# Stick-breaking heads 4 to 6: scores as two matmuls over stacked high and low parts instead of three over masked ones

## The chip, the cores and the metric

The kernel runs on one core of a Trainium2 chip. The metric is the device time of one execution in microseconds. Three timed executions of the kernel before took 2678.01, 2680.74 and 2683.67 us; the median is 2680.74 us. The engines are named as in the profile: PE (matmul; PEld is its weight load), DVE (vector), ACT (scalar), POOL (GpSimd) and SP (the queue from which nearly all transfers are issued).

## The reference, cut to what matters

One layer of a transformer-like block over 2048 rows of width 1024. A normed input is projected; half of the mix is a differential attention with 4 heads, the other half a stick-breaking attention with 8 heads of width 64; then an output projection and a SwiGLU layer follow. The change touches how the scores `z` of the stick-breaking half are formed:

```python
def stick_breaking_attention(q, k, v):
    scale = SB_DIM ** -0.5                       # SB_DIM = 64
    z = jnp.einsum('bqhd,bkhd->bhqk', qb, k).astype(jnp.float32) * scale
    mask = (k_pos[None, :] < q_pos[:, None])[None, None]
    log_1mb = jnp.where(mask, jax.nn.log_sigmoid(-z), 0.0)
    rem = lax.cumsum(log_1mb, axis=3, reverse=True) - log_1mb
    a = jnp.where(mask, jnp.exp(jax.nn.log_sigmoid(z) + rem), 0.0)
    return jnp.einsum('bhqk,bkhd->bqhd', a.astype(v.dtype), v)
...
u = rms_norm(h, norm1_w[l])
proj = jnp.einsum('bsd,de->bse', u, w_in[l])     # diff q|k|v, then stick-breaking q|k|v
...
h = h + jnp.einsum('bse,ed->bsd', mix, w_out[l])
h = h + SwiGLU(rms_norm(h, norm2_w[l]))
```

All is float32. The kernel keeps that precision with float16 matmuls: each operand is split into a high half and a low half (the rounding rest), and a product is the sum of high·high, high·low and low·high.

## The kernel before, in words

The first phase works through eight groups `g` of 128 columns. Groups 0 to 3 are the differential heads, one per group; groups 4 to 7 hold two stick-breaking heads each, `m` = 0 and 1, on the partition halves 0 to 63 and 64 to 127. For each group 16 row tiles are projected (`proj`), and then (`sb_attn`) 16 query tiles `i` run over the keys before them, in chunks `sc` of up to 512 keys, 80 chunks a group. The projections of a group lie beside the attention of the group before it and the first half of its own. A second phase is the SwiGLU layer, which is nearly all matmul.

Groups 4 to 6 are "turned" (`turned(g)`, L330): their q and k leave the projection already transposed, with the 128 columns of both heads on the partitions and the rows along the free side. `proj_turned` (L334) puts q and k of two row tiles into one PSUM tile `pq` and v into `pv`. After each second row tile `turned_out` (L346) evacuates them: for each head q is multiplied by a column of `half`, which is 2^-11 on that head's partitions and zero on the other head's, into a high part (ACT, L350), and DVE takes the low part (L351). k is split once for both heads into high and low (`split_psum`, L359: the high part on ACT or DVE, whichever has the smaller count in `load`; the low part on DVE, L364), and v likewise. Because q is zero on the other head's partitions, a matmul over all 128 partitions gives one head's score. A chunk of scores (`score_chunk`, L504) is then three matmuls into one PSUM bank: q high·k high, q low·k high, q high·k low.

Group 7 and groups 0 to 3 take another way. Their q and k are transposed by transfers (L410), and a second transfer (L412) copies each half of `qT` to the other half of the partitions, so that high and low lie stacked over 128 partitions. For them a chunk of scores is two matmuls.

Behind the scores of a chunk, ACT takes two sigmoids (L619, L620), DVE a running product (L622) and a product (L623, on POOL for every second chunk of a longer row); ACT casts the result to a high half `s` (L89), POOL takes the low half (L98), and a transposing transfer on SP (L461) brings it into `aT`, which is the weight of the value matmuls (L518). The score tiles `sc` have 4 PSUM buffers, `s` has 3 buffers beside two spare kinds, `pq` and `pv` share the 2 buffers of `pj`, `qT` has 4 (`QB`) and `kT` 7 (`KB`).

The order on each engine is not written out. The framework's scheduler sorts all instructions by priority (attention ahead by 200, projection behind by 200) and a modelled course of time; every engine, and SP, then works through its own list in order. So a change in one place moves instructions in others.

## Time and profile before

| | |
|---|---|
| median of three runs | 2680.74 us (2678.01 to 2683.67) |
| span of the profiled execution | 2680.8 us, 50579 instructions |
| attention of groups 4, 5, 6 | about 600 to 757, 757 to 915 and 915 to 1085 us |
| attention of group 7 and part of the output projection | about 1085 to 1355 us |
| second phase | from about 1400 us on |

The span reaches from the first to the last instruction of the profiled execution. The page gives no other time of that execution; its span stands 0.1 us above the median of the timed runs, so nothing is added for what lies around it. The busy time of an engine is the union of its instructions. A matmul's end is modelled: it holds the time until its result is out, while the next matmul starts earlier, so the distance from start to start is what PE needs for one.

### The profile page before, as it was taken

To read this page: it belongs to the slowest core of one execution; us is meant where nothing else is said; L and a number is where in the kernel's file an instruction comes from. 1 tells how busy PE (TensorE), PEld (TensorE's weight loads), DVE (VectorE), ACT (ScalarE), POOL (GpSimd) and SP (SyncE) were. 2 spreads that over 40 slices of the span, in tenths; PEclk is the share of its full clock that TensorE was granted. 3 is DMA by queue.
4 is the path that set the end of the run, shared out by engine and by line. 5 is a ranking of instruction groups with operands and counts; after the bars stand their busy time and mean duration, and the time that the engine had idled before them with its cause. 6 is when DMAs were issued, how large, how long until landed. Compare 5 with 4: busy or idle time off the path is not lost. (4 is left out here: it accounts for less than half of the span.)

```text
span 2680.8 us, 50579 instructions
## 1 busy us (share of the span) xinstructions
PE 2492.4 (93%) x19628; PEld 1498.6 (56%) x19628; DVE 1932.7 (72%) x3711; ACT 1347.0 (50%) x2487; POOL 1489.1 (56%) x1098
## 2 busy tenths in 40 slices
PE   6998989888988989889989899999999999999999
PEld 4655656577776776557775344444444444444444
DVE  6898969898989989877766868777685544444434
ACT  4665656567978878665644535344352112111121
POOL 2578667667767766546764656565564232322323
PEclk9999999999999999999999899999999999999999
DMA  6777697767998979987897574665649743635532
GB/s 222 213 162 181 146 200 168 179 143 184 193 179 179 185 160 209 210 191 217 218 285 282 208 250 178 255 226 202 245 183 346 293 177 143 233 141 186 195 111 95
DMA packets 619585, 534.41 MB, mean 199 GB/s; under 512 B 480640, under 2 KB 548224, under 8 KB 609104
## 3 DMA queue, kind: packets, MB, share of 16 engines
q1 hardware_dynamic: 617520, 529.09, 69.9%
q8 instruction: 154, 2.52, 0.4%
q0 software_dynamic: 512, 1.36, 0.2%
q14 instruction: 87, 0.71, 0.1%
q10 hardware_dynamic: 1312, 0.72, 0.1%
HBM read 261.08 MB, written 147.32 MB: 152 GB/s over the span
## 5 line engine op out<-in xcount | busy, mean ns | idle before, releaser
L98 POOL TENSOR_TENSOR s<-z,s 128x1024 f16<-128x1024 f32 (+7 forms) x288 | 472.0, 1647 | 142.5 <-ACT s L89 109.8
L507 PE MATMUL sc<-kT,qT 128*128 128x512 f16 (+3 forms) x1520 | 382.0, 353 | 53.3 <-DVE z L623 19.3
L622 DVE TENSOR_TENSOR_SCAN z<-z,sc 128x512 f32<-128x512 f32 (+3 forms) x320 | 352.8, 1112 | 58.6 <-ACT sc L620 38.0
L1138 PE MATMUL pd<-wd,act 128*128 128x512 f16 x1764 | 390.9, 379 | 1.2 <-DVE cg L1071 1.2
L326 PE MATMUL pj<-w,xt 128*128 128x384 f16 x1920 | 352.2, 331 | 18.8 <-ACT xt L683 6.9
L1030 PEld LDWEIGHTS <-wg 128*128 128x128 f16 x1848 | 182.0, 99 | 230.2 <-issue 16.4
L518 PE MATMUL yp<-v,aT 128*128 128x64 f16 (+1 forms) x4896 | 269.8, 204 | 41.6 <-DMA aT<-s 40.2
L518 PEld LDWEIGHTS <-aT 128*128 128x128 f16 x4896 | 237.5, 99 | 120.4 <-DMA aT<-s 52.5
L1030 PEld LDWEIGHTS <-wu 128*128 128x128 f16 x1848 | 180.7, 98 | 218.0 <-issue 2.6
L98 POOL TENSOR_TENSOR act<-cg,act 128x512 f16<-128x512 f32 x112 | 148.5, 1337 | 262.9 <-ACT act L1097 150.8
L1138 PEld LDWEIGHTS <-act 128*128 128x128 f16 x1764 | 172.8, 98 | 209.4 <-issue 2.8
L326 PEld LDWEIGHTS <-xt 128*128 128x128 f16 x1920 | 187.3, 99 | 147.5 <-issue 21.4
L89 ACT CAST s<-z 128x128 f16<-128x128 f32 (+7 forms) x215 | 173.1, 809 | 134.1 <-DMA aT<-s 40.5
L98 POOL TENSOR_TENSOR hs<-hs,cu 128x512 f32<-128x512 f32 x99 | 130.9, 1328 | 171.3 <-DVE hs L1144 70.8
L619 ACT ACTIVATE z<-sc,c 128x512 f32<-128x512 f32 (+3 forms) x320 | 210.7, 663 | 25.6 <-PE sc L507 11.7
L1097 ACT CAST act<-cg 128x512 f16<-128x512 f32 x126 | 77.3, 616 | 238.4 <-DVE cg L1103 162.7
L507 PEld LDWEIGHTS <-qT 128*128 128x128 f16 x1520 | 128.4, 99 | 121.0 <-DVE z L623 23.0
L832 PE MATMUL po<-wo,mt 128*128 128x256 f16 x1536 | 180.7, 277 | 13.9 <-DVE xf L835 8.4
L1030 PE MATMUL pm<-X,wu 128*128 128x512 f16 x792 | 180.4, 379 | 1.3 <-DVE wu L221 1.3
L1030 PE MATMUL pm<-X,wg 128*128 128x512 f16 x792 | 181.3, 382 | 0.0
L342 PE MATMUL pj<-xt,w 128*128 128x128 f16 x2304 | 175.0, 220 | 6.7 <-DVE v L364 5.7
L1144 DVE SCALAR_TENSOR_TENSOR hs<-pd,c,hs 128x512 f32<-128x512 f32 x136 | 99.0, 747 | 109.6 <-PE pd L1138 83.1
(266 smaller groups left out, 4737.6 us busy)
## 6 DMA issues: line engine op xcount, KB each, us to landing
xt<-xs SPq DMA_DIRECT2D x112, 512.0 KB, 4.3
hs<-hd SPq DMA_DIRECT2D x68, 512.0 KB, 4.5
hd<-hs SPq DMA_DIRECT2D x56, 512.0 KB, 4.7
split<-wg SPq DMA_DIRECT2D x11, 1792.0 KB, 7.8
split<-wu SPq DMA_DIRECT2D x11, 1792.0 KB, 6.7
split<-wd SPq DMA_DIRECT2D x11, 1792.0 KB, 7.2
wg<-split SPq DMA_DIRECT2D x11, 1792.0 KB, 7.3
wd<-split SPq DMA_DIRECT2D x11, 1792.0 KB, 12.2
```

The lines of the kernel that those rows point to most:

```text
L89: ACT.copy(dst, src)
L98: (DVE if e == "D" else POOL).tensor_tensor(dst, a_, b_, op)
L326: PE.matmul(pj[:, :384], lhsT=xv[:, xi, kt, :], rhs=G["w"][:, wi, kt, :], start=n == 0, stop=n == 23)
L342: PE.matmul(o, lhsT=x_ if c == 2 else w_, rhs=w_ if c == 2 else x_, start=n == 0, stop=n == 23)
L507: last = PE.matmul(sc[:, : 128 * w].rearrange("p (t n) -> p t n", n=P), lhsT=G["q"][i // 4][:, a_, i % 4, :], rhs=G["k"][q][:, b_, 0:w, :] ...
L518: PE.matmul(yp[:, y0 : y0 + wd], lhsT=aT[:, a_, :], rhs=v[:, v_ : v_ + wd], start=start and j == 0 and q == 0, stop=stop and j == nb - 1 a ...
L619: ACT.activation(om[:, lo:hi], sc[:, :w], AF.Sigmoid, scale=G["nkz"][:])
L622: DVE.tensor_tensor_scan(ov, ov, sc[:, :w], om[:, hi : hi + 1], op0=ALU.mult, op1=ALU.bypass)
L832: PE.matmul(po[:, sl], lhsT=mt[:, kt, P * xi : P * xi + P], rhs=wos[2 * h + n][wi][:, kt, :], start=q == 0, stop=q == 23)
L1030: front[0] = PE.matmul(ps_[:].rearrange("p (t n) -> p t n", n=P), lhsT=wv[:, wo, wi, 128 * kt : 128 * kt + 128], rhs=X[xo][:, :, xi, kt, : ...
L1138: front[0] = PE.matmul(po[:], lhsT=act[:, ao, xi, 128 * j : 128 * j + 128], rhs=W["d"][:, wo, wi, :], start=start and u == 0 and q == 0, s ...
L1144: DVE.scalar_tensor_tensor(dst, po[:], kd[:], src, op0=ALU.mult, op1=ALU.add)
```

## The change

`half` goes. `turned_out` splits q and k for each partition half on its own (64 partitions, 256 columns): q high of head `m` to slot `2 + m` of `qT` and q low to slot `m`, k high to slot `m` of `kT` and k low to a new tile `yk`, all on the partitions on which they come out. After the fourth row tile of a batch, six transfers on SP, each 64 partitions by 1 KB, fill the other half of the partitions: k low under k high, q low under q high, q high under q low. `score_chunk` then takes the same two matmuls in all stick-breaking groups: (q high over q low)·(k high over k low), which gives high·high and low·low, and (q low over q high)·(the same), which gives the two mixed products. v is split as before.

```diff
-        half = c1(2, "half")
-        DVE.memset(half[:], 0.0)
-        for m in range(2):
-            DVE.memset(half[64 * m : 64 * m + 64, m : m + 1], 2.0 ** -11)
...
             def turned_out(pq, pv, qT, kT, v, j):
                 two = slice(j - 1, j + 1)
                 q2, k2 = (pq[:, 256 * c : 256 * c + 256].rearrange("p (t n) -> p t n", t=2) for c in range(2))
+                if j == 1:
+                    yk[0] = s16p.tile([P, 4, P], F16, tag="yk", bufs=2, name=nm("yk"))
                 for m in range(2):
-                    ACT.mul(qT[:, m, two, :], q2, half[:, m : m + 1])
-                    DVE.scalar_tensor_tensor(qT[:, 2 + m, two, :], q2, half[:, m : m + 1], qT[:, m, two, :], op0=ALU.mult, op1=ALU.subtract)
-                note("A", 800)
-                note("D", 800)
-                split_psum(kT[:, 0, two, :], kT[:, 1, two, :], k2, 256)
+                    h = slice(64 * m, 64 * m + 64)
+                    split_psum(qT[h, 2 + m, two, :], qT[h, m, two, :], q2[h], 256)
+                    split_psum(kT[h, m, two, :], yk[0][h, two, :], k2[h], 256)
                 vv = v[:, two, :].rearrange("p t (h s e) -> p t h s e", h=2, s=2)
                 split_psum(vv[:, :, :, 0, :], vv[:, :, :, 1, :], pv[:, :256].rearrange("p (t h e) -> p t h e", t=2, h=2), 256)
+                if j < 3:
+                    return
+                for m in range(2):
+                    h, o = slice(64 * m, 64 * m + 64), slice(64 - 64 * m, 128 - 64 * m)
+                    SP.dma_start(kT[o, m].rearrange("p t n -> p (t n)"), yk[0][h].rearrange("p t n -> p (t n)"))
+                    for c in (0, 2):
+                        SP.dma_start(qT[o, 2 - c + m].rearrange("p t n -> p (t n)"), qT[h, c + m].rearrange("p t n -> p (t n)"))
+
+            yk = [None]
...
-            def score_chunk(G, sc, i, q, m, w, cut=False, turned=False):
-                terms = ((m, 0), (2 + m, 0), (m, 1)) if turned else ((2 + m, m), (m, m))
+            def score_chunk(G, sc, i, q, m, w, cut=False):
+                terms = ((2 + m, m), (m, m))
...
-                        front.append(score_chunk(G, sc, i, 2 * b + c, m, w // P, b == i // 8 and hi == n, turned(g)))
+                        front.append(score_chunk(G, sc, i, 2 * b + c, m, w // P, b == i // 8 and hi == n))
```

In the lists of the engines the line numbers of the changed kernel are 4 higher below `turned_out` (L507 is L511, L461 is L465, L622 is L626) and 5 lower above it (L342 is L337). Over the whole program PE has 240 score matmuls fewer (168 of 512 columns and 24 each of 384, 256 and 128) and as many weight loads fewer; SP has 72 transfers more. Of the work of `turned_out`, DVE had 48 low parts of q, 20 high and 24 low parts of k and 15 high parts of v, and now has 48 low parts of q, 48 of k, 22 high parts of q and 15 of k, all on 64 partitions, and no high part of v; ACT had 48 high parts of q, 4 of k and 9 of v, and now has 26 of q and 33 of k on 64 partitions and 24 of v. Of group 7's high parts (`st`) one moves from DVE to ACT. The low parts of v stay on DVE.

Three places of the lists. First DVE, where the second pair of row tiles of batch 3 of group 4 (q and k from `pj_9832`, v from `pj_9833`) is evacuated among running products; before:

```order
L351 SCALAR_TENSOR_TENSOR qT_9395<-pj_9832,half_79,qT_9395 128x256
L363 TENSOR_SCALAR v_9394<-pj_9833 128x4x64
L364 SCALAR_TENSOR_TENSOR v_9394<-pj_9833,v_9394 128x4x64
L622 SCALAR_TENSOR_TENSOR z_10291<-z_10291,sc_10302 128x512
L622 SCALAR_TENSOR_TENSOR z_10325<-z_10325,sc_10327 128x128
L623 TENSOR_TENSOR z_10290<-sc_10302,z_10291 128x512
L610 COPY z_10456<-z_10291 128x1
L351 SCALAR_TENSOR_TENSOR qT_9395<-pj_9832,half_79,qT_9395 128x256
L363 TENSOR_SCALAR kT_9396<-pj_9832 128x256
L364 SCALAR_TENSOR_TENSOR kT_9396<-pj_9832,kT_9396 128x256
```

The same place in the change (there the pair is `pj_9826` and `pj_9827`):

```order
L367 TENSOR_SCALAR qT_9396<-pj_9826 64x256
L481 TENSOR_REDUCE yss_9639<-y_9638 128x8
L627 TENSOR_TENSOR z_9739<-sc_9749,z_9740 128x512
L368 SCALAR_TENSOR_TENSOR qT_9396<-pj_9826,qT_9396 64x256
L367 TENSOR_SCALAR kT_9397<-pj_9826 64x256
L626 SCALAR_TENSOR_TENSOR z_9766<-z_9766,sc_9768 128x384
L368 SCALAR_TENSOR_TENSOR yk_9728<-pj_9826,kT_9397 64x256
L627 TENSOR_TENSOR z_9765<-sc_9768,z_9766 128x384
L612 MEMSET z_9785 128x1
L368 SCALAR_TENSOR_TENSOR v_9395<-pj_9827,v_9395 128x4x64
L491 TENSOR_TENSOR y_9638<-yp_9182,yrs_9642 128x512
L626 SCALAR_TENSOR_TENSOR z_9785<-z_9785,sc_9787 128x384
```

Each evacuation is now of one partition half, and the pieces lie singly between the running products of three chunks; the second half of q and k of this pair comes further down in the list.

Second SP, late in the attention of group 4, at the transfers of `aT` for the same query tiles; before, only the transposes (L461) and the loads of row tiles (`xt`, L424) stand here:

```order
L461 DMA_TRANSPOSE aT_10950<-s_10947 128x14x128
L461 DMA_TRANSPOSE aT_11077<-s_11074 128x16x128
L461 DMA_TRANSPOSE aT_11125<-s_11122 128x16x128
L461 DMA_TRANSPOSE aT_11250<-s_11247 128x16x128
L424 DMA xt_11488<-xs 128x2048
L461 DMA_TRANSPOSE aT_11293<-s_11290 128x16x128
```

In the change five of the six new transfers of one batch (batch 1 of group 5, `qT_10962` and `kT_10963`) stand among them:

```order
L465 DMA_TRANSPOSE aT_11058<-s_11055 128x16x128
L358 DMA qT_10962<-qT_10962 64x512
L465 DMA_TRANSPOSE aT_11104<-s_11101 128x16x128
L356 DMA kT_10963<-yk_11198 64x512
L358 DMA qT_10962<-qT_10962 64x512
L465 DMA_TRANSPOSE aT_11230<-s_11227 128x16x128
L358 DMA qT_10962<-qT_10962 64x512 x2
L428 DMA xt_12213<-xs 128x2048
L465 DMA_TRANSPOSE aT_11271<-s_11268 128x16x128
```

So a transpose of `aT` can now stand behind a transfer that waits for a piece of `turned_out`.

Third PE, at the first score of batch 2 of group 5 (`qT_11873` before, `qT_11848` after); before, the q and k of that batch's second pair of row tiles (`pj_12248`) are projected behind it:

```order
L518 MATMUL yp_12437<-v_10978,aT_12029 128x64
L183 MATMUL wsc_11956<-id_63,m_11958 128x128
L507 LDWEIGHTS qT_11873
L507 MATMUL sc_12538<-kT_11874,qT_11873 128x128
L507 LDWEIGHTS qT_11873
L507 MATMUL sc_12538<-kT_11874,qT_11873 128x128
L342 LDWEIGHTS w_8701
L342 MATMUL pj_12248<-xt_12246,w_8701 128x128
```

In the change:

```order
L522 LDWEIGHTS aT_12001
L522 MATMUL yp_12398<-v_10205,aT_12001 128x64
L511 LDWEIGHTS qT_11848
L511 MATMUL sc_12507<-kT_11849,qT_11848 128x128
L511 LDWEIGHTS qT_11848
L511 MATMUL sc_12507<-kT_11849,qT_11848 128x128
L513 LDWEIGHTS idb
L513 MATMUL sc_12507<-tri,idb 128x128
L522 LDWEIGHTS aT_12001
```

Two score matmuls close the chunk here, with the mask (L513) behind them, where before a third one follows further down. The second pair of the batch is `pj_12215` in the change; the last of its q and k matmuls stands 380 rows ahead of this score in PE's list.

## The prediction, on record before the changed kernel ran

> **What bounds the kernel now.** I read the page first, then the windows of the three groups that the change touches, then who waits for whom in them.
>
> ```profile
> PE 2492.4 (93%) x19628; PEld 1498.6 (56%) x19628; DVE 1932.7 (72%) x3711; ACT 1347.0 (50%) x2487; POOL 1489.1 (56%) x1098
> ```
>
> That is an average over two phases, and it makes PE look like the only bound. The windows cut by groups say more. The boundaries are where the 240 score matmuls of a group begin and end, which the second fence bears out (239, 241 and 243).
>
> ```profile
> core 0: us, PE busy (x) PEld busy (x) DVE busy (x) ACT busy (x) POOL busy (x), PEclk, DMA share, GB/s
> 600.00:757.00 157.00, 139.03 (x2111) 111.99 (x2109) 144.96 (x262) 135.35 (x253) 117.41 (x89) 1.00 0.90 186
> 757.00:915.00 158.00, 141.70 (x2248) 114.53 (x2247) 143.46 (x247) 132.92 (x242) 115.74 (x87) 1.00 0.96 186
> 915.00:1085.00 170.00, 151.01 (x2124) 114.99 (x2120) 149.48 (x270) 132.60 (x241) 116.45 (x90) 0.97 0.91 185
> ```
>
> ```profile
> 600.00:757.00 157.00, 56.67 (x239) 19.05 (x239) 1.00 0.90 186
> 757.00:915.00 158.00, 56.99 (x241) 19.16 (x240) 1.00 0.96 186
> 915.00:1085.00 170.00, 58.35 (x243) 20.84 (x244) 0.97 0.91 185
> ```
>
> In these 485 us DVE is busy for 437.9 us (90.3%; 92.3% in the first window), PE for 431.7 (89.0%), ACT for 400.9 (82.7%), POOL for 349.6, and the transfers for 0.90 to 0.96 of their engines. Nothing is idle for long, and DVE is as full as PE. Who waits, in the same 485 us (us in total, times, longest):
>
> ```profile
> PE yp L518 <- DMA aT<-s: 15.3, 13, 2.3
> PE sc L507 <- DVE z L623: 12.1, 17, 1.6
> PE pj L342 <- DVE v L364: 5.7, 7, 2.3
> ...
> DVE z L622 <- ACT sc L620: 13.3, 16, 3.4
> DVE z L622 <- ACT z L620: 12.9, 8, 4.0
> ...
> ACT s L89 <- DMA aT<-s: 18.0, 11, 3.1
> ...
> ACT z L619 <- PE sc L509: 8.2, 6, 5.5
> ACT qT L350 <- PE pj L342: 7.1, 3, 3.4
> ACT z L619 <- PE sc L507: 6.5, 7, 1.8
> ```
>
> PE waits for DVE to free score buffers and `pj`, and for `aT` to land. DVE's running products wait for ACT's sigmoids, 26.2 us, more than half of DVE's 47 us of idle time. ACT waits for PE 21.8 us (8.2 + 7.1 + 6.5), and 18.0 us for a buffer `s` that a transpose still reads. So it is a ring of equally full engines. I take DVE, the fullest, as the one that sets the pace, and count the time of the stage as DVE's work plus what DVE waits.
>
> **Score matmuls, removed.** Their count by size in the three windows, and trains that show the distance from start to start:
>
> ```profile
> L507 PE MATMUL sc<-kT,qT 128*128 128x512 f16 x506 | 138.4, 384 | 20.8 <-DVE z L623 10.7 <-DVE z L610 4.0 <-DVE z L622 2.9
> L507 PE MATMUL sc<-kT,qT 128*128 128x256 f16 x72 | 11.8, 273 | 1.3 <-DVE z L623 0.7 <-DVE z L622 0.3 <-DVE z L608 0.2
> L507 PE MATMUL sc<-kT,qT 128*128 128x128 f16 x72 | 8.7, 228 | 1.1 <-DVE z L623 0.7 <-DVE kT L363 0.2
> ...
> 783.65 0.82 PE L507 MATMUL sc<-kT,qT 128*128 128x512 f16 x3 [0.59 <-DVE z L608]
> 787.10 0.49 PE L507 MATMUL sc<-kT,qT 128*128 128x256 f16 x3
> 791.88 5.48 PE L342 MATMUL pj<-xt,w 128*128 128x128 f16 x95 [1.18 <-DVE v L364]
> ```
>
> Three of 512 columns take 0.82 us, the last one 0.384 of it, so one costs (0.82 - 0.384) / 2 = 0.218 us. One of 256 costs (0.49 - 0.273) / 2 = 0.109, one of 128 about 5.48 / 95 = 0.058, one of 384, between them, 0.163. The change removes 168 x 0.218 + 24 x (0.163 + 0.109 + 0.058) = 36.6 + 7.9 = 44.5 us of PE, a tenth of what it does here. The weight loads that go with them lie under matmuls.
>
> What that is worth is not 44.5 us. A shorter score helps DVE only through ACT, whose idle time stands before three groups:
>
> ```profile
> L619 ACT ACTIVATE z<-sc,c 128x512 f32<-128x512 f32 (+3 forms) x238 | 158.2, 671 | 15.0 <-PE sc L509 8.2 <-PE sc L507 6.5
> L89 ACT CAST s<-z 128x1024 f16<-128x1024 f32 (+7 forms) x142 | 117.7, 834 | 53.2 <-DMA aT<-s 18.0 <-DVE z L623 9.1 <-issue 9.0
> ...
> L350 ACT ACTIVATE qT<-pj,half 128x256 f16<-128x256 f32 x42 | 21.7, 518 | 11.7 <-PE pj L342 7.1 <-DVE qT L351 4.5
> ```
>
> Of these 15.0 + 53.2 + 11.7 = 79.9 us PE causes 21.8, or 27%. 27% of the 26.2 us that DVE waits for ACT is 7 us; 27% of all of DVE's idle 47 us is 13. I take 10, between them. The bounds are 0 (what is behind PE in the ring is late anyway) and 44.5 (PE alone sets the pace).
>
> **The evacuation, split by halves.** The rows of the operations, and a pair that shows how DVE's instructions overlap:
>
> ```profile
> L351 DVE SCALAR_TENSOR_TENSOR qT<-pj,half,qT 128x256 f16<-128x256 f32 x43 | 20.3, 473 | 1.8 <-ACT qT L350 1.6
> L364 DVE SCALAR_TENSOR_TENSOR kT<-pj,kT 128x256 f16<-128x256 f32 x22 | 9.1, 413 | 0.3
> L363 DVE TENSOR_SCALAR kT<-pj 128x256 f16<-128x256 f32 x20 | 8.3, 413 | 0.0
> L361 ACT ACTIVATE kT<-pj x4: 373/380/384, 564.4 to 618.1; 128x256 f16<-128x256 f32 x4
> ...
> 791.43 0.40 DVE L364 SCALAR_TENSOR_TENSOR v<-pj,v 128x256 f16<-128x256 f32 x1
> 791.74 0.47 DVE L351 SCALAR_TENSOR_TENSOR qT<-pj,half,qT 128x256 f16<-128x256 f32 x1
> ```
>
> The second starts 0.09 us before the first ends, so an instruction costs DVE its duration less 0.09: 0.38 us for a low part of q with `half`, 0.32 for the forms with a constant. [...] Before: 48 x 0.38 + (20 + 24 + 15) x 0.32 = 18.2 + 18.9 = 37.1 us. After: (48 + 48 + 22 + 15) x 0.32 = 42.6. DVE gets 5.5 us more, and as the pace-setter it pays all of it. If 64 partitions took half (0.21 - 0.09 each), DVE would save 21 us. ACT (its high part of q is the row L350 above): 48 x 0.518 + 13 x 0.38 = 29.8 before, 83 x 0.38 = 31.5 after; 1.7 us on an engine with 84 us idle, taken as 0 (at most 1.7). The three memsets of `half` at the start cost nothing that is waited for.
>
> **The small transfers, added.** The nearest rows are the copies L412 of groups 0 to 3 and 7, which move 64 partitions by 2 KB: issue times, who waited, and the landing. The last two rows are the transfers' load in the 485 us, and a window of the second phase.
>
> ```profile
> L412 SPq DMA_DIRECT2D qT<-qT x40: 467/576/1759, 75.6 to 1186.8; - x40
> ...
>   PEld L507: 5.1, 2
>   PE sc L507: 4.8, 3
> ...
> DMA to landing us min/median/max: 2.2/2.4/4.6
> ...
> q1 hardware_dynamic: 240501, 88.93, 91.3%
> ...
> 2200.00:2300.00 100.00, 100.00 (x465) 45.30 (x464) 42.06 (x55) 18.25 (x29) 29.40 (x24) 1.00 0.48 175
> ```
>
> SP pays 72 x 0.576 = 41 us of issuing over 485 us. On the 16 engines a transfer of 65.5 KB takes 0.18 us at the second phase's rate (175 GB/s at 0.48) and 0.32 us at this stage's (88.93 MB in 485 us is 183 GB/s, at 0.913): 13 to 23 us, 3 to 5% of the 443 us now used. The waits for `aT` and for `s` (15.3 + 18.0 us) hang on those engines and on SP; 5% of 33.3 us is 1.7, and I charge 1. The bounds are 0 and 10 us: a third more on those waits, if the queue grows faster than its load.
>
> A batch's scores now wait for a landing where before they waited for DVE. In groups 0 to 3 and 7 PE lost 4.8 us to L412 over 20 batches, 0.25 us a batch; 12 batches would make 3 us. I charge 0, because the projection is moved ahead: where before the second pair of batch 2 of group 5 was projected behind the batch's first score, its matmuls now end 380 rows (190 matmuls, over 10 us at 0.058) ahead of it, against 2.4 us of landing and some 3 us of splits. If that cover is gone, it costs the 2.4 us and those 3 us each time, and behind the waiting score on PE stand value and projection matmuls of other tiles. Behind a new transfer that waits on SP stand transposes of `aT`, which the value matmuls need only five to seven stages (one or two chunks each) later.
>
> [...]
>
> **The sum.** -10 (DVE waits less) + 5.5 (DVE works more) + 1 (transfers) = -3.5 us, on 2680.8: **2677 us**. What is won in these groups moves all that follows forward, since group 7 and the second phase start behind them.
>
> **Rivals.**
>
> *PE sets the pace after all.* For it: PE is as full as DVE, and it works in order, so scores stand behind projections. Against: 12.1 us of PE's waits are for DVE to free a score buffer. It gives what DVE allows: DVE's 443.4 us of work at 96% busy, which no window here reaches, is 462 us instead of 485, so -23 us: 2658 us.
>
> *Slower: DVE is delayed at each change of the partition half.* Every running product starts on partition 0, every second evacuation now on partition 64, alone between products. If DVE lets an instruction that starts on another part of the partitions begin only when the one before has ended, each such start loses the 0.09 us of overlap. About 66 of the 133 pieces start on partition 64, and the instruction behind each changes back: 132 x 0.09 = 12 us of DVE. Then DVE has 437.9 + 5.5 + 12 = 455 us of work; at its best share, 92.3%, that is 493 us, +8, and at today's mean, 90.3%, 504. It makes the kernel slower as soon as these delays exceed the 3.5 us above. I put it at +10: 2691 us. [...] No row here starts on partition 64 in a loop, so the trace can't say yet.
>
> *Late transfers.* The transfers come late at the starts of batches, or SP gets in the way of `aT`. The nearest rows bound it by 12 x 2.4 = 29 us; at a third of that, less the relief, +5: 2686 us.
>
> *The change doesn't do what it says.* The lists show 240 score matmuls fewer, so that much is done.
>
> **How the numbers follow.** Forecast 0.51, PE's pace 0.20, halves on DVE 0.17, late transfers 0.12. What a measurement of this kernel can tell from no change is about 0.2%, 5.4 us: faster means below 2675.4, slower above 2686.2. The forecast's own range is -14 to +6 (relief of 3 to 20, the other terms as bounded nearby): 0.20 faster, 0.27 same, 0.04 slower. PE's pace is faster, 0.20. Halves: 0.03 same, 0.14 slower. Late transfers: 0.03 and 0.09. Together 0.40, 0.33 and 0.27. For the range I leave out the far half of the first rival and the far end of the slower ones: 2657 to 2695.
>
> **What would show it.** Right: the three groups take 475 to 485 us; DVE's busy share rises to 91 to 93% while PE's falls to about 82%; `z L619` waits less for `sc`. A low part of 64 partitions lasts 0.41 us on DVE. Rival one: DVE above 94%. The halves: starts on partition 64 no longer overlap with the instruction before, and DVE's work grows by more than 10 us. Late transfers: waits of `sc` for `qT` or `kT` transfers of over 5 us, or `yp` waiting for `aT` well over 15 us. Wrong altogether if group 7 or the second phase changes its length, by the new order rather than by the scores.

## The result, and the profile after

The changed kernel takes 2710.1 us (median of four runs, 2708.19 to 2713.77); the kernel before, timed beside it, takes 2681.6 (2678.01 to 2683.67). The ratio is **1.0117, with a 95% interval of 1.0101 to 1.0132**: slower by 28 us by the medians and 31 by the ratio. The forecast was 2677 and its range ended at 2695, so the sign and the range were both wrong. The profiled execution spans 2707.5 us, 26.7 more than the one before.

The page's line of engines, after. The 240 matmuls are gone, and PE's busy time falls by 21 us; DVE's grows by 10.9 us and ACT's by 11.6:

```profile
PE 2471.4 (91%) x19388; PEld 1492.6 (55%) x19388; DVE 1943.6 (72%) x3733; ACT 1358.6 (50%) x2510; POOL 1490.7 (55%) x1098
```

The windows after, one for each of groups 4 to 7. They are cut where a group's 80 running products begin (L626 here, L622 before); the columns are those of the prediction's windows:

```profile
603.00:797.00 194.00, 150.89 (x2353) 128.67 (x2351) 159.82 (x281) 146.69 (x273) 122.36 (x93) 0.94 0.86 172
797.00:964.00 167.00, 139.71 (x2259) 119.30 (x2260) 148.39 (x261) 136.46 (x249) 116.57 (x87) 0.94 0.96 188
964.00:1132.00 168.00, 133.89 (x1715) 95.54 (x1713) 150.31 (x268) 133.79 (x244) 120.00 (x89) 0.93 0.94 193
1132.00:1381.00 249.00, 219.91 (x2343) 173.72 (x2341) 197.19 (x344) 163.49 (x299) 146.26 (x102) 0.96 0.91 210
```

Cut in the same way, the kernel before has groups of 160.5, 158.8, 170.8 and 260.7 us. So group 4 loses 34, group 5 loses 8, group 6 wins 2, and group 7, in which the change alters no more than the engine of one high part, wins 11.5. The second phase is as long as it was (1326.0 against 1326.3). DVE, which the prediction wanted to see at 91 to 93% in these groups, is at 82% of group 4 (159.82 of 194). PE's granted clock, 1.00 in two of the three groups before, is 0.93 to 0.94.

The four lengths don't hold the same work, because the new order brings projections forward. The projection matmuls in group 4, before (L342) and after (L337), as busy time of PE and of its weight load with their counts:

```profile
603.70:764.20 160.50, 70.33 (x1110) 63.55 (x1110) 1.00 0.90 185
602.80:797.40 194.60, 87.46 (x1320) 81.69 (x1320) 0.94 0.86 172
```

These 210 more are some 12 us of PE, by the prediction's 0.058 us for one. Group 6 has 512 of them instead of 793. So group 4's 34 us are not all waiting, and group 6's 2 us are not all won.

Who waits, in the 529 us of groups 4 to 6 after (us in total, times, longest):

```profile
PE yp L522 <- DMA aT<-s: 32.8, 29, 2.7
DVE z L626 <- ACT sc L624: 19.4, 18, 3.1
PE sc L511 <- DVE z L626: 18.1, 20, 2.7
ACT z L623 <- PE sc L513: 16.9, 11, 3.3
PE sc L511 <- DVE z L627: 14.2, 14, 3.5
...
DVE z L626 <- ACT z L624: 8.9, 11, 2.9
...
ACT z L623 <- PE sc L511: 5.5, 7, 1.9
...
PE sc L511 <- DMA qT<-qT: 4.8, 4, 2.8
PE sc L511 <- DMA kT<-yk: 2.6, 1, 2.6
```

PE's waits for `aT` have doubled (15.3 before), and scores wait 7.4 us for the new transfers: both are what the prediction named as signs of the rival "late transfers". DVE's waits for ACT's sigmoids, which the forecast wanted to shrink, are 28 us (19.4 + 8.9), as before (26.2). ACT's waits for scores are up from 14.7 to 22.4 (16.9 + 5.5).

Two places in group 4 show how such a wait comes about. At the first, twelve transposes take up 26.5 us of SP's list, and the six transfers of batch 1 stand behind them. SP is not busy all that time: between 600 and 645 us it waits 20.9 us for POOL, which makes the low halves that the transposes move (L98).

```profile
611.05 26.54 SPq L465 DMA_TRANSPOSE aT<-s  x12
632.49 0.43 DVE L368 SCALAR_TENSOR_TENSOR yk<-pj,kT 64x256 f16<-64x256 f32 x1 [1.53 <-ACT kT L365]
637.69 0.54 SPq L356 DMA_DIRECT2D kT<-yk  x1
640.36 0.45 PE L511 MATMUL sc<-kT,qT 128*128 128x128 f16 x2 [2.75 <-DMA qT<-qT]
641.41 0.37 ACT L623 ACTIVATE z<-sc,c 128x128 f32<-128x128 f32 x1 [3.08 <-PE sc L513]
642.07 0.48 DVE L626 TENSOR_TENSOR_SCAN z<-z,sc 128x128 f32<-128x128 f32 x1 [2.95 <-ACT z L624]
```

The last low part of k is done at 632.92, but its transfers start at 637.69; then PE, ACT and DVE each wait some 3 us. At the second place, batch 2, the score waits again, and PE goes on with projections, not scores, while DVE has nothing to do:

```profile
673.87 1.94 PE L337 MATMUL pj<-xt,w 128*128 128x128 f16 x27 [4.13 <-DVE v L368]
...
680.11 0.37 PE L511 MATMUL sc<-kT,qT 128*128 128x128 f16 x2 [2.59 <-DMA kT<-yk]
...
682.57 2.76 PE L337 MATMUL pj<-w,xt 128*128 128x128 f16 x24
...
685.13 2.96 PE L337 MATMUL pj<-xt,w 128*128 128x128 f16 x48
...
688.12 0.42 DVE L367 TENSOR_SCALAR qT<-pj 64x256 f16<-64x256 f32 x1 [6.00 <-PE pj L337]
```

In these rows stands the clock too: the row of 24 projection matmuls lasts 2.76 us, 0.115 for each, and a little later one of 48 lasts 2.96, 0.062 for each. The granted clock is 1.00 from 671.8 to 675.1 us and 0.50 from 675.2 to 685.3.

That looked like an answer, the queue on SP. The experiments say that it is the smaller part of it.

### The profile page after: what moved, and what is told of

It reads as the page before. It is cut to its first block, busy times and chain, and to the rows that moved or that the text cites. A ratio compares the mean times of both kernels' runs of the same rounds, so it can differ in the third digit from the quotient of the medians.

```text
span 2707.5 us, 50281 instructions
## 1 busy us (share of the span) xinstructions
PE 2471.4 (91%) x19388; PEld 1492.6 (55%) x19388; DVE 1943.6 (72%) x3733; ACT 1358.6 (50%) x2510; POOL 1490.7 (55%) x1098
## 4 chain that ended last, share of the span: by engine, by line
PE 43%; DVE 13%; issue 5%; DMA 4%; POOL 4%; ACT 3%; SPq 0%; DVEq 0%; ACTq 0%; POOLq 0%
PE pd L1142 14%; PE pm L1034 10%; PE pd L1034 7%; PE pa L1034 6%; DVE z L626 4%; DMA aT<-s 3%; PE po L836 3%; POOL s L98 1%; DVE wd L216 1%; DVE z L627 1%; PE pj L337 1%; DVE wu L216 1%; ACT z L623 1%; ACT s L89 1%; ACT sc L624 1%
## 5 line engine op out<-in xcount | busy, mean ns | idle before, releaser
L98 POOL TENSOR_TENSOR s<-z,s 128x1024 f16<-128x1024 f32 (+7 forms) x288 | 474.1, 1656 | 141.6 <-ACT s L89 124.3
L511 PE MATMUL sc<-kT,qT 128*128 128x512 f16 (+3 forms) x1280 | 344.5, 359 | 74.4 <-DVE z L627 19.2
L626 DVE TENSOR_TENSOR_SCAN z<-z,sc 128x512 f32<-128x512 f32 (+3 forms) x320 | 354.0, 1112 | 55.8 <-ACT sc L624 38.6
L321 PE MATMUL pj<-w,xt 128*128 128x384 f16 x1920 | 354.3, 332 | 11.1 <-ACT raw L379 4.8
L522 PEld LDWEIGHTS <-aT 128*128 128x128 f16 x4896 | 236.9, 100 | 158.6 <-DMA aT<-s 92.9
L98 POOL TENSOR_TENSOR act<-cg,act 128x512 f16<-128x512 f32 x112 | 148.5, 1335 | 263.1 <-ACT act L1101 150.9
L321 PEld LDWEIGHTS <-xt 128*128 128x128 f16 x1920 | 187.3, 99 | 140.8 <-issue 19.4
L98 POOL TENSOR_TENSOR hs<-hs,cu 128x512 f32<-128x512 f32 x99 | 130.8, 1329 | 171.4 <-DVE hs L1148 70.8
L623 ACT ACTIVATE z<-sc,c 128x512 f32<-128x512 f32 (+3 forms) x320 | 203.6, 640 | 28.7 <-PE sc L513 19.0
L337 PE MATMUL pj<-xt,w 128*128 128x128 f16 x2304 | 175.6, 229 | 11.7 <-DVE v L368 4.7
L511 PEld LDWEIGHTS <-qT 128*128 128x128 f16 x1280 | 105.8, 100 | 121.8 <-DVE z L627 23.8
```

The lines of the kernel that those rows point to most:

```text
L98: (DVE if e == "D" else POOL).tensor_tensor(dst, a_, b_, op)
L321: PE.matmul(pj[:, :384], lhsT=xv[:, xi, kt, :], rhs=G["w"][:, wi, kt, :], start=n == 0, stop=n == 23)
L337: PE.matmul(o, lhsT=x_ if c == 2 else w_, rhs=w_ if c == 2 else x_, start=n == 0, stop=n == 23)
L511: last = PE.matmul(sc[:, : 128 * w].rearrange("p (t n) -> p t n", n=P), lhsT=G["q"][i // 4][:, a_, i % 4, :], rhs=G["k"][q][:, b_, 0:w, :] ...
L522: PE.matmul(yp[:, y0 : y0 + wd], lhsT=aT[:, a_, :], rhs=v[:, v_ : v_ + wd], start=start and j == 0 and q == 0, stop=stop and j == nb - 1 a ...
L623: ACT.activation(om[:, lo:hi], sc[:, :w], AF.Sigmoid, scale=G["nkz"][:])
```

## The experiments

For each run the length of the groups was read from its trace, which is of one execution. e13, which differs from the kernel before only from group 4 on, starts that group 3.7 us earlier, so a difference of less than some 4 us says nothing. All ratios are to the kernel before, timed beside it on the same chip; the intervals are of 95%.

| run | median us | ratio (interval) | start of group 4 | group 4 | 5 | 6 | 7 |
|---|---|---|---|---|---|---|---|
| before | 2681.6 | 1 | 603.7 | 160.5 | 158.8 | 170.8 | 260.7 |
| the change | 2710.1 | 1.0117 (1.0101, 1.0132) | 602.8 | 194.6 | 166.5 | 168.5 | 249.2 |
| e1 | 2744.3 | 1.0243 (1.0221, 1.0265) | 600.0 | 180.1 | 175.3 | 191.7 | 252.5 |
| e2 | 2729.8 | 1.0180 (1.0163, 1.0197) | 604.6 | 178.2 | 175.6 | 183.2 | 263.4 |
| e3 | 2718.5 | 1.0137 (1.0122, 1.0152) | 605.0 | 164.9 | 182.4 | 169.6 | 265.4 |
| e4 | 2711.2 | 1.0108 (1.0093, 1.0123) | 604.5 | 163.6 | 162.5 | 186.3 | 258.4 |
| e5 | 2693.7 | 1.0029 (1.0017, 1.0040) | 599.9 | 158.6 | 163.0 | 176.5 | 265.4 |
| e6 | 2716.2 | 1.0107 (1.0088, 1.0127) | 617.1 | 159.6 | 166.2 | 187.5 | 257.7 |
| e7 | 2728.4 | 1.0161 (1.0145, 1.0176) | 604.9 | 192.7 | 169.0 | 171.5 | 263.7 |
| e8 | 2760.5 | 1.0283 (1.0265, 1.0301) | 622.6 | 187.4 | 182.5 | 173.0 | 261.3 |
| e9 | 2734.9 | 1.0197 (1.0175, 1.0219) | 602.0 | 195.3 | 168.9 | 177.4 | 258.2 |
| e10 | 2713.5 | 1.0115 (1.0097, 1.0134) | 608.4 | 180.2 | 160.9 | 167.4 | 269.3 |
| e11 | 2704.9 | 1.0080 (1.0062, 1.0098) | 602.4 | 169.8 | 162.2 | 168.3 | 269.4 |
| e12 | 2733.5 | 1.0184 (1.0159, 1.0209) | 605.1 | 185.3 | 177.2 | 182.9 | 254.3 |
| e13 | 2676.8 | 0.9977 (0.9966, 0.9989) | 600.0 | 159.0 | 161.5 | 168.5 | 256.6 |
| e14 | 2680.2 | 0.9985 (0.9972, 0.9998) | 602.4 | 167.3 | 156.3 | 166.2 | 263.1 |
| e15 | 2718.7 | 1.0129 (1.0107, 1.0150) | 603.5 | 171.9 | 170.6 | 187.4 | 258.6 |
| e16 | 2734.4 | 1.0190 (1.0171, 1.0210) | 601.5 | 185.3 | 181.0 | 184.1 | 251.4 |
| e17 | 2713.2 | 1.0118 (1.0095, 1.0140) | 602.5 | 168.0 | 168.3 | 187.2 | 257.0 |
| e18 | 2687.7 | 1.0024 (1.0009, 1.0040) | 600.4 | 164.5 | 162.0 | 173.9 | 262.3 |

### First round: parts undone or done alone (e1 to e4)

**e1**: no transfers; three score matmuls over the head's 64 partitions. The edit is shown against the change, without the lines of the transfers, which go.

```diff
-                    split_psum(kT[h, m, two, :], yk[0][h, two, :], k2[h], 256)
+                    split_psum(kT[h, m, two, :], kT[h, 1 - m, two, :], k2[h], 256)
...
+                terms = ((2 + m, m), (m, m), (2 + m, 1 - m)) if turned else ((2 + m, m), (m, m))
+                h = slice(64 * m, 64 * m + 64) if turned else slice(0, P)
```

> Evacuation by partition halves as in the change, but no transfers: a head's score is three matmuls over that head's 64 partitions (high-high, low-high, high-low), the low part of k lying in the free half of kT. Queue theory (the loss comes from small transfers that stand behind transposes on SP while the scores wait for them): the loss goes, 2678 to 2692 us. Splits theory (twice as many, half as wide evacuations hold DVE and ACT): 2700 us or more. Transfer-load theory (72 transfers load SP and the DMA engines, whoever waits): 2678 to 2690.

**e2**: the same with the first two of these terms.

> As the kernel with three matmuls over 64 partitions, without high-low, which is left out of the result: two matmuls a chunk as in the change, and no transfers. Queue theory: what the shorter scores are worth alone shows, 2664 to 2680 us. Splits theory: 2695 or more. Transfer-load theory: as the queue theory.

**e3**: group 4 as in the kernel before, groups 5 and 6 as in the change. **e4**: the kernel before, and 72 transfers of the new size that nothing reads.

```diff
+                if masked:
+                    ...
+                    split_psum(kT[:, 0, two, :], kT[:, 1, two, :], k2, 256)
-                terms = ((2 + m, m), (m, m))
+                terms = ((m, 0), (2 + m, 0), (m, 1)) if masked else ((2 + m, m), (m, m))
```

```diff
+                if j == 3:
+                    for c in range(6):
+                        h, o = slice(64 * (c % 2), 64 * (c % 2) + 64), slice(64 - 64 * (c % 2), 128 - 64 * (c % 2))
+                        yk = s16p.tile([P, 4, P], F16, tag="yk", bufs=2, name=nm("yk"))
+                        SP.dma_start(yk[o].rearrange("p t n -> p (t n)"), (qT[h, c] if c < 4 else kT[h, c - 4]).rearrange("p t n -> p (t n)"))
```

> Group 4 as before (masked q, three matmuls, no transfers), groups 5 and 6 as in the change. Queue theory, with the loss at batches 1 and 2 of group 4: 2676 to 2692 us, at least 18 less than the change. Splits theory and transfer-load theory, which put a third of the loss in each group: 2698 to 2704.

> The kernel before, with 72 transfers of the same size from the same halves of qT and kT to a tile that nobody reads, six after each batch, on SP. Queue theory: the scores do not wait for them, 2678 to 2690 us. Transfer-load theory: 2700 or more. Splits theory: 2678 to 2686.

None of the four is near the kernel before. e1 and e2 can't be used for the evacuation, because a matmul over 64 partitions brought a price of its own: PE's busy time is 2541.1 us in e1, 48.7 more than in the kernel before with as many matmuls, and 2516.7 in e2, 45 more than in the change with as many. From start to start, a projection matmul that a 64-row score follows took 0.152 us in these runs instead of 0.056, and a 64-row score that a 128-row matmul follows 0.308 instead of 0.216: 0.09 us for each change of the number of rows. e4 came out as the theory of the transfers' load had it (2700 or more), e3 in no theory's range. e3 is the odd one: with group 4 the old way, group 4 is nearly as short as before (164.9), and the loss is in group 5 (182.4), where the change alone loses 8. In e4 it lies in group 6. The loss moves about, in part with the projections, and does not stay with the part that is changed.

### Second round: the same work in another order (e5 to e8)

So these four change no work (e5 moves one or two evacuations from DVE to ACT), only numbers that the order follows from: **e5** (kernel before) the counts by which the program balances ACT and DVE, **e6** (kernel before) the priority of the evacuation, **e7** (the change) that of the attention, **e8** (the change) that of the evacuation.

```diff
-                note("A", 800)
-                note("D", 800)
+                note("A", 700)
+                note("D", 900)
```

```diff
-PRI = {"sc": 0, "spl": 0, "pv": 0, "fin": 0, "pm": -200, "po": 0, ..., "at": 200, "ox": 0, "wm": 0}
+PRI = {"sc": 0, "spl": 0, "pv": 0, "fin": 0, "pm": -200, "po": 10, ..., "at": 200, "ox": 0, "wm": 0}
```

> The kernel before with the same work, instructions and transfers; only the planner's counts of a masked evacuation change, ACT 800 to 700 and DVE 800 to 900, which moves a few evacuations between ACT and DVE and with them the scheduler's order of groups 4 to 7. Order theory (the time of these groups hangs on how well the scheduled order fits, the order of the kernel before fits unusually well, and whatever disturbs it costs 15 to 40 us): 2693 to 2720 us. Queue theory and splits theory: nothing changed that they speak of, 2675 to 2687 us.

> The kernel before with one priority changed (evacuations of the projection 0 to 10), so the same work in another order. Order theory: 2693 to 2720 us. Queue and splits theory: 2672 to 2690 us.

> The change with the priority of attention 190 instead of 200: the same work in a slightly other order. Order theory: anywhere from 2685 to 2730 us, at least 6 us away from the change as likely as not. Queue theory and splits theory: 2703 to 2717 us, as the change.

> The change with the priority of the projection's evacuations 10 instead of 0, as in the run of the kernel before with it. Order theory: 2685 to 2730 us, and not slower than the kernel before with the same priority by 28 us but by -10 to 15. Queue theory: transfers come a little earlier, 2695 to 2712 us, and 28 us or a little less above the kernel before with the same priority. Splits theory: 2705 to 2715 us, 28 above it.

On the kernel before, e5 costs 0.3% and e6 1.1%; on the change, e7 costs 18 us more than the change itself and e8 50 by the medians, 12 and 45 by the ratios. e6 and e8 already lose 13 and 20 us ahead of group 4 (their evacuations of groups 0 to 3 move too), and e6 loses 17 in group 6. With equal work an order can cost as much as the whole change does. That is a size, though, not yet the cause. And the order theory missed once: e8 stands 44 us above e6, where it had said -10 to 15.

### Third round: queue, lead, transfers, clock (e9 to e12)

**e9**: the new transfers from GpSimd's queue. **e10**: the projection of groups 4 to 6 a batch further ahead. **e11**: no transfers, and evacuations over all 128 partitions; its scores leave out q high·k low and take in the other head's columns. **e12**: the first score matmul twice, the second time over the first.

```diff
-                    SP.dma_start(kT[o, m].rearrange("p t n -> p (t n)"), yk[0][h].rearrange("p t n -> p (t n)"))
+                    POOL.dma_start(kT[o, m].rearrange("p t n -> p (t n)"), yk[0][h].rearrange("p t n -> p (t n)"))
```

```diff
-  int(NT * (g + 1 + fr) - (LAG * (1 - LF * fr * (g == NG - 1)) if g else ...
+  int(NT * (g + 1 + fr) - ((LAG - 4 * (3 <= g < 6)) * (1 - LF * fr * (g == NG - 1)) if g else ...
```

```diff
-                    split_psum(qT[h, 2 + m, two, :], qT[h, m, two, :], q2[h], 256)
-                    split_psum(kT[h, m, two, :], yk[0][h, two, :], k2[h], 256)
+                    split_psum(qT[:, 2 + m, two, :], qT[:, m, two, :], q2, 256)
+                    split_psum(kT[:, m, two, :], yk[0][:, two, :], k2, 256)
...
-                if j < 3:
-                    return
-                for m in range(2):
-                    ...
```

```diff
-                terms = ((2 + m, m), (m, m))
+                terms = ((2 + m, m), (2 + m, m), (m, m)) if turned else ((2 + m, m), (m, m))
...
```

> The changed kernel with its 72 small transfers issued by GpSimd instead of SyncE, so that none of them stands behind a transpose of aT in SyncE's list. Queue theory (scores of batches 1 and 2 of group 4 wait for transfers that stand behind up to 26 us of transposes): group 4 comes down from 194.6 us to about 165, and the whole to about 2682, within 0.3% of the kernel before. Order theory (what costs is that the order of all engines from group 4 on is another, and no longer fits): 2700 to 2725, whichever group it falls on. Load theory (the 72 transfers themselves delay the transposes and loads, whatever queue): about 2710, with waits for aT as long as in the changed kernel.

> The changed kernel with the projection of groups 4 to 6 one batch of four rows further ahead of the attention than now. Queue theory: the transfers of batches 1 and 2 of group 4 land before their scores are due, group 4 comes to about 165 us and the whole to about 2685. Order theory: 2700 to 2730. If the lists of SyncE still put the transfers behind the transposes, then about 2710.

> The changed kernel without its 72 transfers: the evacuations are made over all 128 partitions instead of over the two halves, the same number of them and with the same number of columns, so that both blocks are there for the scores without a transfer. It leaves out the small product of the high part of q and the low part of k, and adds the other head's columns; PE's work, DVE's and ACT's are those of the change. If the transfers (their queue or their load) cost the 28 us: 2675 to 2685, and group 4 at 160 to 165 us. If the relief of PE is given back by its clock or by another order: 2700 to 2725, with 0.97 to 0.98 of the clock.

> The changed kernel with the first of the two score matmuls of groups 4 to 6 issued twice, the second time over the first, so that PE has three matmuls for each chunk as in the kernel before, beside the new evacuations and transfers. Clock theory (PE with less to do idles more, and its clock is granted at half for it): the clock comes back to 0.984 and the time is no longer than that of the change, 2700 to 2712. Queue theory: PE's saving was worth little, so 2710 to 2725. If PE's saving did bring what was forecast (10 us) or more and something else took it: 2720 to 2750.

The queue theory falls as the cause of the whole: in e9 a score waits for a new transfer only once, 0.7 us, and group 4 still takes 195.3 us, with PE's waits for `aT` as long as in the change (34.8 us). The whole, 2734.9, is above every forecast made for e9; the new issues also cost POOL 37 us of busy time (1527.6 against 1490.7), a load that the change doesn't have. In e10 group 4 wins 14 us, and group 7 gives 20 back. e11, with no transfer and no piece on a half of the partitions, is still 1.0080: a loss of 21 to 24 us comes about without any transfer. Between e11 and the change lie 5 us by the medians and 10 by the ratios, but the two also differ in their order (group 4 is 25 us shorter in e11, group 7 20 longer), so this is not the transfers' price. The clock theory falls with e12, which has PE's old work and a clock of 0.981, and is 23 us slower than the change, not as fast. I read that as PE's relief being worth 23 us. The next round shows that this was wrong.

### Fourth round: the lists kept (e13 to e18)

All runs so far changed the order along with the work, so they measure both at once. Here the two are taken apart. In e13, e16, e17 and e18 the program is ordered first, and then single instructions are taken out of the finished lists, put in or shortened; every other instruction of every engine stands where it stood. The matmuls taken out carry no wait and no signal; their weight loads stay (PEld x19628 in e13 and e16).

**e13** is the kernel before without the second of its three score matmuls, q low·k high; **e14** the same work, ordered anew and without those weight loads; **e15** e11 with the first matmul twice, so the new evacuation alone; **e16** e12 with the second copies taken out.

```diff
     with tile.TileContext(nc, schedule_with_timeline_sim=True) as tc:
         block(tc, aps, o[0])
+    for bb in nc.main_func.blocks:
+        kept = [i for i in bb.instructions if i.name not in dropped]
+        if len(kept) < len(bb.instructions):
+            bb.instructions = kept
...
```

```diff
-                terms = ((m, 0), (2 + m, 0), (m, 1)) if turned else ((2 + m, m), (m, m))
+                terms = ((m, 0), (m, 1)) if turned else ((2 + m, m), (m, m))
```

> The kernel before, with the second of the three score matmuls of groups 4 to 6 taken out of the finished lists, so that every engine's list is that of the kernel before but for these 240 matmuls. It leaves out the product of the low part of q and the high part of k. This is the relief of PE alone, in the old order. My sum took 10 us for it (bounds 0 to 44.5); the run with the first matmul issued twice suggests 23. If PE's relief is worth what it is in that run: 2655 to 2661. If it is given back by the clock of an idler PE: 2676 to 2684, with a clock under 0.98.

> The same work as in the run before, but written with two matmuls from the start, so that the lists of all engines are made anew (it leaves out the same product). Order theory (a list made anew costs 10 to 40 us whatever is changed, because the numbers in the kernel were set for the old one): 15 to 40 us longer than the run with the old order kept, 2670 to 2700. If the order is not what costs: within 8 us of it.

> The run without transfers (full evacuations in four pieces more) with the first score matmul issued twice, so PE has three matmuls as before: the new evacuations alone, in an order made anew. It leaves out the same product as the run without transfers. My sum took 5.5 us for the evacuations: 2686 if the order costs nothing. Order theory: 2700 to 2730 (2705 of the run without transfers, and up to 23 us for the matmuls). What is above 2700 here is the evacuations and the order together; the run with two matmuls in the old kernel says how much of it an order can be.

> The run with the first score matmul issued twice, with the second copies taken out of the finished lists: the changed kernel's whole work, in the order made for three matmuls. Relief theory (240 matmuls are worth the same in any order): 20 to 25 us below that run's 2733, so 2708 to 2713. If that run's 23 us were the order's: anywhere from 2700 to 2733, and 2733 if PE's relief is worth nothing.

Taking 240 matmuls out of lists that stay as they are brings **0.23% (0.11 to 0.34), or 6 us**, in the kernel before, and nothing in e16 (2734.4 against e12's 2733.5). So the 23 us between e12 and the change were the order's, as the last sentence of e16's expectation allowed, and PE's relief is worth 0 to 6 us. (e16 keeps the 240 weight loads. Nothing speaks for a price of theirs: e13, which keeps them too, is no slower than e14, which doesn't.) The order made anew in e14 costs some 3 us beside e13: a new order need not be a bad one, and the order theory's 15 to 40 us for any new order were wrong. In e14 the projections stand as far forward as in the change (1343 matmuls in group 4, 471 in group 6), and its group 4 takes 167.3 us: that they move forward doesn't by itself make 194.6. But e15, the evacuation alone, costs 1.29%, 35 us. Is that the work of two more pieces for each pair of tiles, or their order? **e17** takes e15's lists and makes two of the eight q and k pieces 2 columns wide, so that six full ones are left, as before. **e18** takes the lists of the kernel before and makes each part of k twice, so that there are eight.

```diff
+        bb.instructions = [copy.replace(i, ins=tuple(narrow(a) for a in i.ins), outs=tuple(narrow(a) for a in i.outs)) if i.name in short else i for i in bb.instructions]
```

```diff
+        bb.instructions = [j for i in bb.instructions for j in ([again(i, r0), i] if i.name in longer else [i])]
```

> The run with the evacuation alone, with its lists kept and the two low parts of k that nothing reads made on 2 columns instead of 256. So each pair of tiles has six full pieces for q and k, as in the kernel before, and PE's three matmuls, in the order that was made for eight pieces (it leaves out the same product as the run without transfers). If the work of the new pieces costs the 35 us: 2685 to 2695. If the order made for them costs it: 2708 to 2718, 16 us less work on DVE notwithstanding. Between 2695 and 2708 both count.

> The kernel before, with its lists kept and each high and low part of k of groups 4 to 6 made twice (the first time into a spare buffer), 44 more pieces of 256 columns on DVE and 4 on ACT: the number of pieces of the changed kernel, in the old order. My sum's rule (DVE pays every microsecond of its own work, 0.32 us for each piece): 14 us more than the kernel before, 2696. Work theory, going by the run with the evacuation alone: 2710 or more. Order theory: 2682 to 2692, since DVE has idle time in the old order that takes the pieces in.

The pages' lines of engines, of e17 and of e18:

```profile
PE 2511.3 (92%) x19628; PEld 1514.5 (56%) x19628; DVE 1928.7 (71%) x3733; ACT 1350.2 (50%) x2510; POOL 1489.3 (55%) x1098
```

```profile
PE 2494.8 (93%) x19628; PEld 1498.9 (56%) x19628; DVE 1947.1 (72%) x3756; ACT 1348.0 (50%) x2491; POOL 1490.3 (55%) x1098
```

e17 has as many matmuls as the kernel before and 4 us less on DVE (1928.7 against 1932.7), and takes **1.0118 (1.0095 to 1.0140)**, 32 us more. e18 has 14 us more on DVE, more than the change adds, and takes **1.0024 (1.0009 to 1.0040)**, 6.5 us more. What comes with the lists made for the new pieces is what costs; their work is a fifth of it. Beside the order, e17's lists keep eight pieces (two of them short) with their waits, and 23 instructions more than before on ACT (x2510 against x2487); these were not taken apart from the order.

What is worse in that order? Waits in groups 4 to 6, of e17 and then of e18 (L617 and L622 are the running product, L614 and L619 the first sigmoid, L615 and L620 the second, L502 and L507 the score, L504 and L509 the mask that closes it, L356 and L358 high parts):

```profile
DVE z L617 <- ACT sc L615: 36.3, 29, 3.5
ACT z L614 <- PE sc L504: 24.8, 15, 7.1
PE yp L513 <- DMA aT<-s: 21.5, 18, 2.2
DVE z L617 <- ACT z L615: 18.0, 14, 3.0
PE sc L502 <- DVE kT L358: 7.4, 5, 2.6
PE sc L502 <- ACT kT L356: 6.9, 3, 2.8
```

```profile
DVE z L622 <- ACT z L620: 13.1, 7, 5.0
DVE z L622 <- ACT sc L620: 11.3, 14, 3.3
PE yp L518 <- DMA aT<-s: 10.5, 9, 2.8
ACT z L619 <- PE sc L507: 9.7, 7, 3.9
ACT z L619 <- PE sc L509: 8.3, 7, 5.9
```

DVE waits for sigmoids 54 us in e17 and 24 in e18, PE for `aT` 21.5 and 10.5, ACT for a score 25 (one of these waits is 7.1) and 18, and scores wait directly for high parts of k 14 us in e17 and 0.6 in e18. One such place in e17's timeline:

```profile
872.94 1.27 DVE L617 TENSOR_TENSOR_SCAN z<-z,sc 128x512 f32<-128x512 f32 x1
...
874.13 0.40 DVE L358 TENSOR_SCALAR qT<-pj 128x256 f16<-128x256 f32 x1
874.44 1.27 DVE L617 TENSOR_TENSOR_SCAN z<-z,sc 128x512 f32<-128x512 f32 x1
875.63 0.40 DVE L359 SCALAR_TENSOR_TENSOR qT<-pj,qT 128x256 f16<-128x256 f32 x1
875.95 0.41 DVE L358 TENSOR_SCALAR kT<-pj 128x256 f16<-128x256 f32 x1
...
876.42 0.34 PE L502 MATMUL sc<-kT,qT 128*128 128x128 f16 x3 [2.62 <-DVE kT L358]
...
876.85 0.37 ACT L614 ACTIVATE z<-sc,c 128x128 f32<-128x128 f32 x1 [2.42 <-PE sc L504]
```

A running product of 1.27 us stands in DVE's list between two pieces of one evacuation, and a score, with the projections behind it, waits for the last of them. Worked out over the 24 pairs of tiles of each run, the time from the first q or k piece of a pair to its last is on average 7.7 us in the kernel before, 8.4 in e18 and 9.3 in e14, but 10.9 in e17, 11.1 in e15 and 12.0 in the change. Among these six the runs that spread the pieces further are the slow ones. The other runs don't bear it out: e4 and e6 have 7.9 and 7.8 us and are as slow as the change (2711.2 and 2716.2), and e11 has 12.6 and is faster than e12 with 11.4 (2704.9 and 2733.5). So the spread doesn't tell a slow order from a fast one.

## Why the prediction was wrong, point by point

**The step that failed** is the one that is missing from "The sum": three terms were added as if every other instruction stayed where it was. The prediction says in its last sentence on what would show it that a changed group 7 would mean the new order at work; group 7 did change (260.7 to 249.2), but the sum had no term and no rival for it. It also saw the projections move ahead, and drew from that only that the transfers are covered. With the lists kept, the terms come out small, as forecast: -6 for the relief (e13), and for the pieces some 5 (an estimate: the change's 10.9 us more on DVE at the 0.45 that e18 gives). That leaves nearly all of the 28 us for the order, the holds on DVE at a change of the partition half (below) and the transfers. For the new evacuation without transfers e17 shows what its lists cost, 32 us. For the change itself the order's part is not shown in the same way, since its transfers and pieces can't be put into the old lists; it is what is left over.

**The relief, taken as -10.** Measured are -6 (-9 to -3) in the old order and 0 in e12's. So the term was too large, and the path given for it is not seen: shorter scores were to spare ACT waits for PE, and so DVE waits for ACT. e13, in the 485 us of the prediction's waits (600 to 1085):

```profile
PE sc L507 <- DVE z L623: 15.8, 18, 1.7
...
DVE z L622 <- ACT sc L620: 14.2, 17, 2.9
...
DVE z L622 <- ACT z L620: 12.7, 8, 4.8
```

DVE waits for ACT 26.9 us (26.2 before), and ACT for scores 13.4 (14.7 before). What PE gains it waits for DVE to free a score buffer, 43 us in all instead of 23. Groups 4 to 6 take 489.0 us in this execution and took 490.1. The rival "PE sets the pace" (-23) is out.

**The evacuation, taken as +5.5.** The rows of the changed kernel (DVE, by form):

```profile
L368 DVE SCALAR_TENSOR_TENSOR qT<-pj,qT 64x256 f16<-64x256 f32 x48 | 20.0, 417 | 3.5 <-ACT qT L365 2.4
L368 DVE SCALAR_TENSOR_TENSOR yk<-pj,kT 64x256 f16<-64x256 f32 x48 | 19.8, 413 | 5.3 <-ACT kT L365 4.5
L367 DVE TENSOR_SCALAR qT<-pj 64x256 f16<-64x256 f32 x22 | 8.9, 406 | 11.2 <-PE pj L337 11.1
L367 DVE TENSOR_SCALAR kT<-pj 64x256 f16<-64x256 f32 x15 | 6.1, 405 | 0.0
```

No row of the kernel before has such a piece over 64 partitions; the sum's 0.32 us for one came from rows over 128. Here such a piece lasts 0.405 to 0.417 us, where the two forms of k over 128 partitions took 0.413 before, so the 0.41 us held. What was wrong is "as the pace-setter it pays all of it": in e18 DVE's work grows by 14.4 us and the time by 6.5, so a microsecond of DVE's work costs 0.45 (the interval of e18's ratio is 2 to 11 us, 0.17 to 0.74).

**DVE held at each change of the partition half, a rival with 12 us.** No row of the kernel before starts on partition 64 in a loop, so the prediction put it as an if; the trace of the change shows the delay. Rows of DVE's timeline, first two pieces on partition 0 (head 0; the row does not name the half, the program's order of pieces does), then a piece on partition 64 (the low part of k of head 1) between two products:

```profile
672.76 0.40 DVE L368 SCALAR_TENSOR_TENSOR qT<-pj,qT 64x256 f16<-64x256 f32 x1
673.09 0.40 DVE L367 TENSOR_SCALAR kT<-pj 64x256 f16<-64x256 f32 x1
...
695.98 1.27 DVE L626 TENSOR_TENSOR_SCAN z<-z,sc 128x512 f32<-128x512 f32 x1
697.28 0.43 DVE L368 SCALAR_TENSOR_TENSOR yk<-pj,kT 64x256 f16<-64x256 f32 x1
697.74 1.28 DVE L626 TENSOR_TENSOR_SCAN z<-z,sc 128x512 f32<-128x512 f32 x1
```

The piece at 673.09 starts 0.07 us ahead of the end of the one before it. The piece at 697.28 starts 0.03 behind the end of the product, and the next product 0.03 behind the end of the piece. In the whole trace none of the 50 pieces on partition 64 overlaps with its predecessor and none of their followers on another half with them, and 45 of the 55 pieces on partition 0 behind other work do. 85 such starts on another half come right behind the instruction before (within 0.12 us); at 0.11 us each (0.03 late instead of 0.08 early) that is 9 us of DVE, and at e18's 0.45 about 4 us of time, an estimate. It was not tried alone. e11 and the change differ by it, by the transfers and by their order, and in all by 5 to 10 us.

**The transfers, taken as +1, and late ones as 0.** The step "I charge 0, because the projection is moved ahead" was worked out on group 5 and taken for all. In groups 5 and 6 it nearly held: one score waited, 1.6 us. At batches 1 and 2 of group 4 the scores did wait, 2.75 and 2.59 us: at batch 1 the transfers stood behind transposes on SP, at batch 2 four of them, issued from 673.88 us on, took 4.8 to 5.9 us to land. Over the whole run a new transfer landed 2.8 us after its issue at the median (1.9 to 6.3), where the copies L412 took 2.4 before (2.2 to 4.6). The waits and the doubled waits for `aT` look like the rival "late transfers". That they are the whole of the 28 us is ruled out by e11, which has no transfer and loses 21 to 24; what they cost in the change itself is not shown. In e4, 72 idle transfers on the kernel before cost 1.08%, more than between e11 and the change; how much of that is their load and how much the order was not taken apart.

**What stays open**: which property of an order makes it slow. The loss moved from group to group between runs with nearly the same work, and one such run (e14) lost nothing. Neither the place of the projections (e14) nor the spread of the pieces (e4, e6) nor the mean clock (e12, below) tells the slow orders from the fast.

## What to carry to other kernels

Where a scheduler makes the order anew after every edit, an edit has two prices, its work and its order, and a sum of terms prices only the first. Measure them apart: take instructions out of the finished lists or put them in, and compare that with the kernel ordered anew. Here the work came to about nothing (-6 and some +5) and the lists made for the new pieces to some 30 us (e17). So before an edit of this size is judged, several orders of each version should be timed.

In this ring of engines, 83 to 90% busy before, neither relief nor load counted in full: 27 us less on PE's busy time (2465.7 in e13) brought 6 us, and 14 us more on DVE cost 6.5.

## What the runs showed of the hardware that was not expected

- Matmuls over 64 and over 128 partitions in turn: each change between them took PE 0.09 us in e1 and e2, 0.152 instead of 0.056 and 0.308 instead of 0.216 from start to start. The price shows in e1, where PE is busy 48.7 us longer than in the kernel before with as many matmuls, and in e2, 45 us longer than in the change; twice 0.09 us for each of 240 chunks would be 43.
- Behind PE's wait of 4.13 us in group 4 the granted clock was 0.50 from 675.2 to 685.3 us, and the matmuls took 0.115 us instead of 0.062, the rows shown above. The clock was still 1.00 when the wait ended at 673.87, and fell 1.2 us later, after a stretch (671.8 to 675.1) in which PE was busy for 1.23 us. Over the whole run the clock was 0.976 against 0.984 before, 0.984 in e18 and 0.981 in e13. It doesn't by itself tell the time: e14 has 0.977 with the change's count of matmuls and takes 30 us less than the change, and e12 has 0.981 and takes 23 more. I read it as following the waits; that was not tried alone.
